# Quarters of the up weights by plain loads with their sums on VectorE, and the last pass's pairs one iteration later

## The chip, the cores and the metric

The kernel runs on one core of one Trainium2 chip. The metric is the device time of one execution in microseconds, the median of several runs. TensorE (PE) multiplies, VectorE (DVE) and ScalarE (ACT) do elementwise work, GpSimd (POOL) does small work and issues some DMAs, SyncE (SP) issues most DMAs.

## The reference

Two layers of a decoder trunk on 512 tokens with a model width of 1024, all in float32. Each layer adds a mixer of four branches (their projections, an indexer with sparse attention, an mLSTM, a gating unit, a short convolution) to `x`, and then an MLP with a hidden width of 4096:

```python
def squared_relu_mlp(h, w_up, w_down):
    return jnp.square(jax.nn.relu(h @ w_up)) @ w_down

def reference(x, ln_mix, w_in, ...):
    for l in range(DEPTH):
        h = rms_norm(x, ln_mix[l])
        x = x + hybrid_mixer(h, pos, w_in[l], ...)
        h = rms_norm(x, ln_mlp[l])
        x = x + squared_relu_mlp(h, w_up[l], w_down[l])
    return x
```

The change lies mostly in `h @ w_up`, with a small part in the projections of the mixer.

## The kernel before, in words

**Split products.** Every float32 matrix is split into a high part (`hi`, a copy to fp32r) and a low part (`lo`, the rest). A product takes three matmuls: high by high, high by low, low by high (`mm3`, L268). For weights, `split_w` (L258) does this: ScalarE copies the raw weights to `whi` and VectorE subtracts to get `wlo`. There are two raw buffers (tag `raw`) and three each of `whi` and `wlo` (`WB`, L34). A raw buffer is free for the next load when both parts are made.

**Order of the work.** The kernel is unrolled by a scheduler, which places each engine's instructions in one fixed queue by priority and by its own idea of when inputs are ready. Loads of weights, splits, sums and the copies out of PSUM have high priority, so they run as far ahead as buffers allow. On the chip each queue is run strictly in order: an instruction that waits holds up all behind it. A plain dependency for order alone can be added by hand (`tc.add_manual_dep` with `V._dep`): it fixes a place in the schedule and adds no wait of its own between instructions of one engine.

**The MLP.** `mlp` (L389) takes the 4096 hidden columns in four passes of 1024. A pass has an up stage of four iterations `t` (L489), each for 256 hidden columns, and a down stage. An up iteration is either plain (two chunks of 128 columns by `next_w`, L246, 48 products of 128x128 by 512 tokens, L498) or by seven products (`up_seven`, L417): the 2x2 blocks of weights and of `h` are combined as in Winograd's form of Strassen's scheme, so that seven half-sized products take the place of eight. `SEVEN` (L38) says which iterations of each pass are done so: (2, 3), (1, 3), (1, 3), (0, 2). In what follows such an iteration is called a pair.

**A pair.** The four quarters of the pair's weights are B11, B12, B21 and B22, each 128x512 floats (256 KB), in DRAM one behind the other. They and their sums stand in four buffers `R[0]` to `R[3]` (tag `cr`, six buffers of 128x1024 in all, L39 and L407), each with a lower and an upper half. Before the change, B11 is loaded twice, B22 twice, B21 once, all on SyncE's queue (L430), and B12 twice by DMAs on GpSimd's queue that add to what is already there (L428). VectorE makes two sums (L442, L449). `form` (L445) splits a buffer when its first product is due, multiplies, and VectorE and ScalarE combine the results in PSUM into `F` (L457 to L484). `F` is then combined again and split into `ah` and `al` (L506 to L513) for the down stage. The down stage (L531 to L745) uses the same six buffers: two for a chain of sums, two for B22, two for a sum of two blocks. Its first loads are tied to `early`, the last product of iteration 0 (L494). In passes 1 to 3 its results are added to partial sums in DRAM by GpSimd's DMAs (L568).

**The mixer's start.** The second projection (L930) leaves four PSUM banks, which ScalarE copies to `sm` and `qe`, eight copies with a factor `rs` (L933 to L937). Its results and those of the first projection (`qiT`, transposed at L975) share the same PSUM banks. Then comes the third projection, whose four chunks of weights are split by `next_w`.

Nearly all instructions show line 143, a helper that records them, so groups are told apart by the names of their tiles: `up` for products of the up stage, `q` and `r` for those of the down stage, `tk` for token projections, `cr` for the buffers above, `U` for the combinations in a pair, `co` for results of the down stage.

Of the kernel before, what the change touches and what calls it, by code (L numbers as in the profile page):

```python
# [16 lines left out]
AF = mybir.ActivationFunctionType  # L17
ALU = mybir.AluOpType
# [16 lines left out]
G1K = ((1, 1, 2, 2, 2), (2, 2, 2, 2))  # L35
KORD = ((0, 1, 2, 3, 4, 5, 6, 7), (4, 5, 6, 7, 0, 1, 2, 3))
PASSES = (8, 8, 8, 8)
SEVEN = ((2, 3), (1, 3), (1, 3), (0, 2))  # L38
CRB = 6  # L39
BIG = 1e30  # L40

# [12 lines left out]
def chunk_plan(l):  # L54
# [30 lines left out]
    for p, nt in enumerate(PASSES):  # L85

        half = nt // 2 * P
        for t in range(0, half, P):
            parts = 2 if t // P in SEVEN[p] else 1
            for i in range(parts):  # L90
# [76 lines left out]
def ins_of(r):  # L167
    return getattr(r, "ins", r)


def trunk(tc, x_in, wall, consts, lps, sgus, out):
    nc = tc.nc
    at = dict(mm=None, side=False, first=None)
    V, S, G, T_ = (Paced(tc, e, at) for e in (nc.vector, nc.scalar, nc.gpsimd, nc.tensor))
    HP = lambda off=URGENT: tc.high_priority(offset=off)
    plan = [ch for l in range(NL) for ch in chunk_plan(l)]
    with ExitStack() as es:
# [80 lines left out]
        def split_w(raw, L, n, copy=S.copy):  # L258
            hi = wpool.tile([P, WCH], F32R, name="whi", tag="whi", bufs=WB[1])
            lo = wpool.tile([P, WCH], F32R, name="wlo", tag="wlo", bufs=WB[1])  # L260
            with HP():
                copy(hi[:, :L], raw[:, :L])
                r = V.tensor_sub(lo[:, :L], raw[:, :L], hi[:, :L].bitcast(F32))
            at["first"] = r if pos[0] == 1 else None
            return (hi[:, :L].rearrange("p (k n) -> p k n", n=n),
                    lo[:, :L].rearrange("p (k n) -> p k n", n=n))
# [17 lines left out]
        side = []  # L284
# [104 lines left out]
        def mlp(l, hh, hl, r2, gain, fp, sh, sl):  # L389
# [9 lines left out]
            sums = sum_dram[l]  # L399
            with tc.tile_pool(name="ap", bufs=1) as ap:  # L400
# [6 lines left out]
                def cr():  # L407
                    return ap.tile([P, 1024], F32, name="cr", tag="cr", bufs=CRB)
# [8 lines left out]
                def up_seven(F):  # L417

                    base, sz = off[0], P * 512
                    off[0] += 4 * sz  # L420
                    pos[0] += 4

                    def ld(dst, i, j, add=False):
                        o = base + ((i - 1) * 2 + j - 1) * sz
                        src = wall[o:o + sz].rearrange("(p l) -> p l", l=512)
                        with HP():
                            if add:
                                nc.gpsimd.dma_start(dst, src, accum_op=ALU.add)  # L428
                            else:
                                nc.sync.dma_start(dst, src)  # L430

                    R = [cr() for _ in range(4)]
                    lo, up = slice(0, 512), slice(512, 1024)
                    ld(R[0][:, up], 1, 1)
                    ld(R[0][:, up], 1, 2, True)
                    ld(R[0][:, lo], 1, 1)
                    ld(R[1][:, up], 2, 2)
                    ld(R[2][:, lo], 2, 2)
                    ld(R[2][:, lo], 1, 2, True)
                    ld(R[3][:, lo], 2, 1)  # L440
                    with HP():
                        V.tensor_add(R[1][:, lo], R[0][:, up], R[1][:, up])  # L442
                    ws = [None] * 4

                    def form(f, o, i, n, first=True):  # L445
                        if ws[i] is None:
                            if i == 2:
                                with HP():
                                    V.tensor_add(R[2][:, up], R[1][:, lo], R[3][:, lo])  # L449
                            ws[i] = split_w(R[i], 512 if i == 3 else 1024, P)  # L450
                        w_h, w_l = ws[i]
                        for k in range(4):
                            bh, bl = moving(f, k)
                            mm3(o, w_h[:, 4 * n + k], w_l[:, 4 * n + k], bh, bl, first and k == 0, k == 3, not first)
                        tick()

                    A, B, C, E = (mmtile("up", "ms")[:, 0:256] for _ in range(4))  # L457
                    s1, s2 = (hpool.tile([P, 2, 256], F32, name="U", tag=n) for n in ("acc", "sq"))
                    U, U2, W, R5 = s1[:, 0], s1[:, 1], s2[:, 0], s2[:, 1]
                    form(A11, A, 0, 0)  # L460
                    with HP():
                        S.copy(U, A)
                    form(S1, B, 0, 1)
                    with HP():
                        S.copy(R5, B)
                    form(S2, C, 1, 0)
                    with HP():
                        V.tensor_sub(U2, C, U)
                    form(S4, B, 1, 1, False)
                    with HP():  # L470
                        V.tensor_add(F[:, A12], B, U2)
                    form(S3, C, 2, 0, False)
                    with HP():
                        V.tensor_sub(W, C, U)
                        V.tensor_add(F[:, A22], W, R5)
                        S.activation(F[:, 2:4], F[:, 2:4], AF.Relu)
                    form(A22, E, 2, 1)
                    with HP():
                        V.tensor_sub(F[:, A21], E, W)
                        S.activation(F[:, A21], F[:, A21], AF.Relu)  # L480
                    form(A12, A, 3, 0, False)
                    with HP():
                        S.activation(F[:, A11], A, AF.Relu)
                        S.activation(F, F, AF.Square)  # L484

                for p, nt in enumerate(PASSES):
# [44 lines left out]
                    nkp, base, sz = nk // 2, off[0], P * 1024  # L531
# [113 lines left out]
                    for k in range(nkp):  # L645
                        raw = wpool.tile([P, WCH], F32, name="raw", tag="raw", bufs=WB[0])
# [54 lines left out]
                    for k in range(nkp):  # L701
                        raw = wpool.tile([P, WCH], F32, name="raw", tag="raw", bufs=WB[0])
# [25 lines left out]
                    for b in range(2):  # L728
                        for qs in ((0,), (1,)) if final and b else ((0, 1),):
                            o = slice(qs[0] * 256, qs[-1] * 256 + 256)  # L730
# [5 lines left out]
                            c, a = c11[b][:, o], bank[b][:, o]  # L736
# [18 lines left out]
        for l in range(NL):  # L755
# [13 lines left out]
            if nxt:  # L769
                hh, hl = nxt  # L770
                rs, rb = rstd(acc, l + 1, 8)
# [3 lines left out]
def mixer(tc, em, env):  # L775
    nc = tc.nc
    HP = lambda off=URGENT: tc.high_priority(offset=off)
# [7 lines left out]
    def et(name):  # L785
        return yp.tile([P, T], F32, name=name, tag="e", bufs=8)
# [14 lines left out]
    if l > 0:  # L801
        rs, rb = env["rs"], env["rb"]
# [86 lines left out]
    else:  # L889
# [28 lines left out]
        rs, rb = rstd(acc[0], 0)  # L918
# [11 lines left out]
    psm = tok_proj(336, 2, range(4), ["mm", "ms", "ms", "ms"])  # L930
    sm = tt([P, 320], "sm").rearrange("p (c w) -> p c w", c=4)
    qe = [et("qe0"), et("qe1")]
    for c in range(4):  # L933
        with HP():
            S.activation(sm[:, c], psm[c][:, 0:80], AF.Identity, scale=rs[:, c:c + 1])
            S.activation(qe[c // 2][:, (c % 2) * 256:(c % 2) * 256 + 256], psm[c][:, 80:336], AF.Identity,
                         scale=rs[:, c:c + 1])  # L937
    rsh = tt([P, 4], "rsh")
    V.tensor_scalar(rsh, rs, 0.5, None, ALU.mult)

# [405 lines left out]
    for c in range(4):  # L1346
        with HP():
            S.activation(ke[c // 2][:, (c % 2) * 256:(c % 2) * 256 + 256], kvp[c][:, 0:256], AF.Identity,
                         scale=rs[:, c:c + 1])
# [38 lines left out]
    for c in range(4):  # L1388
        with HP():
            S.activation(v2[c // 2][:, (c % 2) * 256:(c % 2) * 256 + 256], pav[c][:, :256], AF.Identity,  # L1390
                         scale=rs[:, c:c + 1])
    vs = tt([P, 4], "vs")
    for c2 in range(2):
        t = et("gv")
        gelu2(v2[c2], t)
        for j in range(2):
            s_ = slice(j * 256, j * 256 + 256)
            c = c2 * 2 + j
# [202 lines left out]
```

## Time and profile before

| | |
|---|---|
| runs | 1639.28, 1639.61 and 1641.83 us, median 1639.61 |
| profiled execution | 1638.28 us, span 1636.5 us |
| granted TensorE clock | 0.991 |
| busy | PE 1588.2, DVE 1221.8, ACT 757.4, POOL 170.9 us |
| idle time of VectorE until a quarter landed | 89.7 us in 22 waits |
| DMA | 230.81 MB, mean 141 GB/s |

In a row of a group stand the line, engine, operation, out<-in with shapes and the count, then busy time in us and the mean duration in ns, then the engine's idle time just before these instructions and what ended it. In a row of a timeline stand the start and duration in us, and in brackets the idle time before and what ended it. In a row of waits stand who waited for whom, then us in total, times, and the longest. In a row of DMA issues stand count, KB each, and median us from issue to landing. SPq and POOLq are the queues that issue DMAs.

### The profile page before, as it was taken

The numbers are of one execution on the slowest core, as the hardware profiler recorded it, in microseconds if no ns is written. First come the engines' busy times: TensorE is split into PE (matmuls) and PEld (weight loads), VectorE is DVE, ScalarE is ACT, GpSimd is POOL, SyncE is SP. The second block draws the span as 40 slices with busy tenths as digits, with TensorE's granted clock in tenths as the row PEclk, the third lists the DMA queues.
The fourth block names the chain that finished last, engine by engine and source line by source line (L and its number), as shares of the span: only waits on it lengthen the run. The fifth ranks groups of instructions, "written<-read, shape, count | busy, mean of one in ns | idle before, by whom it ended". The sixth has DMA issues, their size and how long they took to land.

```text
span 1636.5 us, 22046 instructions
## 1 busy us (share of the span) xinstructions
PE 1588.2 (97%) x8163; PEld 1329.5 (81%) x8163; DVE 1221.8 (75%) x2095; ACT 757.4 (46%) x1168; POOL 170.9 (10%) x219
## 2 busy tenths in 40 slices
PE   9899999999998999989999999999999999989798
PEld 7788888888887787878888878878888788878687
DVE  6799997555578686766978999965556686857678
ACT  4554224423356474645545433254234564636363
POOL 1221000000001012121013110000000010021210
PEclk9999999999999999999999999999999999999999
DMA  7433322322366677768445233223223567686892
GB/s 176 135 89 109 101 96 97 117 96 93 110 185 174 186 187 171 202 149 259 133 126 149 79 111 104 81 97 132 97 88 127 160 189 202 165 174 167 167 283 78
DMA packets 85323, 230.81 MB, mean 141 GB/s; under 512 B 9664, under 2 KB 17024, under 8 KB 85216
## 3 DMA queue, kind: packets, MB, share of 16 engines
q1 hardware_dynamic: 63664, 179.74, 33.5%
q0 software_dynamic: 20688, 48.66, 15.9%
q8 instruction: 64, 1.05, 0.3%
q10 hardware_dynamic: 864, 1.01, 0.2%
q14 instruction: 43, 0.35, 0.1%
HBM read 204.69 MB, written 21.01 MB: 138 GB/s over the span
## 4 chain that ended last, share of the span: by engine, by line
PE 53%; DVE 21%; issue 11%; DMA 10%; ACT 4%; POOL 1%; SPq 0%; DVEq 0%; POOLq 0%; ACTq 0%
PE up L143 15%; PE g L143 14%; DMA cr<-in_wall_dram 7%; DVE wlo L143 6%; PE tk L143 6%; PE wo L143 4%; PE p L143 4%; PE q L143 3%; DVE sco L143 3%; PE fm L143 2%; PE r L143 2%; ACT whi L143 2%; DVE m L143 2%; DMA sum_dram<-co 1%; DVE Fs L143 1%
## 5 line engine op out<-in xcount | busy, mean ns | idle before, releaser
L143 ACT CAST whi<-raw 128x1024 fp32r<-128x1024 f32 (+3 forms) x204 | 224.2, 1100 | 224.0 <-DMA raw<-in_wall_dram 70.3
L143 DVE TENSOR_TENSOR wlo<-raw,whi 128x1024 fp32r<-128x1024 f32 (+3 forms) x205 | 262.8, 1283 | 32.4 <-ACT whi L143 30.3
L143 DVE TENSOR_TENSOR wlo<-cr,whi 128x1024 fp32r<-128x1024 f32 (+1 forms) x144 | 166.5, 1161 | 55.2 <-ACT whi L143 55.1
L143 PE MATMUL g<-hh,whi 128*128 128x512 f32 x512 | 200.6, 392 | 0.0
L143 PE MATMUL g<-hh,wlo 128*128 128x512 f32 x512 | 199.5, 390 | 0.0
L143 PE MATMUL g<-hl,whi 128*128 128x512 f32 x512 | 199.3, 389 | 0.0
L143 ACT CAST whi<-cr 128x1024 fp32r<-128x1024 f32 (+1 forms) x144 | 144.4, 1004 | 115.3 <-PE r L143 44.1
L143 PE MATMUL up<-hh,whi 128*128 128x512 f32 (+1 forms) x448 | 155.6, 347 | 5.2 <-DVE co L143 5.2
L143 PE MATMUL up<-hh,wlo 128*128 128x512 f32 (+1 forms) x448 | 155.1, 346 | 2.7 <-DVE wlo L143 2.7
L143 PE MATMUL up<-hl,whi 128*128 128x512 f32 (+1 forms) x448 | 155.0, 346 | 0.0
L143 ACT ACTIVATE gs<-gs 128x512 f32<-128x512 f32 x64 | 40.6, 634 | 201.3 <-DVE gs L143 201.2
L143 DVE TENSOR_TENSOR cr<-cr 128x512 f32<-128x512 f32 (+1 forms) x48 | 41.6, 867 | 95.5 <-DMA cr<-in_wall_dram 89.7
L143 PEld LDWEIGHTS g<-hh,wlo 128*128 128x128 f32 x512 | 96.1, 188 | 20.5
L143 PEld LDWEIGHTS g<-hh,whi 128*128 128x128 f32 x512 | 96.1, 188 | 19.8 <-issue 0.2
L143 PEld LDWEIGHTS g<-hl,whi 128*128 128x128 f32 x512 | 96.2, 188 | 19.1
L143 PE MATMUL tk<-whi,hh 128*128 128x512 f32 (+2 forms) x304 | 108.7, 361 | 0.0
L143 PE MATMUL tk<-wlo,hh 128*128 128x512 f32 (+2 forms) x304 | 107.7, 356 | 0.0
L143 PE MATMUL tk<-whi,hl 128*128 128x512 f32 (+2 forms) x304 | 106.8, 354 | 0.0
L428 POOL DMA_DIRECT2D cr<-in_wall_dram x32 | 28.1, 879 | 720.5 <-DMA cr<-in_wall_dram 567.8
L143 DVE TENSOR_TENSOR gs<-g,rb 128x512 f32<-128x512 f32 x64 | 44.1, 689 | 78.8 <-PE g L143 78.7
L143 PE MATMUL q<-wlo,ah 128*128 128x512 f32 (+1 forms) x260 | 100.1, 389 | 0.7 <-DVE wlo L143 0.7
L143 PE MATMUL q<-whi,ah 128*128 128x512 f32 (+1 forms) x260 | 100.5, 392 | 0.0
(309 smaller groups left out, 3759.6 us busy)
## 6 DMA issues: line engine op xcount, KB each, us to landing
raw<-in_wall_dram SPq DMA_DIRECT2D x131, 512.0 KB, 3.9
raw<-in_wall_dram SPq DMA_DIRECT2D x64, 640.0 KB, 3.8
cr<-in_wall_dram POOLq DMA_DIRECT2D x48, 512.0 KB, 7.2
cr<-in_wall_dram SPq DMA_DIRECT2D x80, 256.0 KB, 4.1
cr<-in_wall_dram SPq DMA_DIRECT2D x32, 512.0 KB, 4.3
cr<-in_wall_dram POOLq DMA_DIRECT2D x32, 256.0 KB, 4.5
sum_dram<-co POOLq DMA_DIRECT2D x32, 256.0 KB, 7.3
x<-in_x_dram SPq DMA_DIRECT2D x16, 256.0 KB, 5.0
```

Of the source, the lines that this page charges most:

```text
L143: r = f(*a, **k)
L428: nc.gpsimd.dma_start(dst, src, accum_op=ALU.add)
```

## The change

- The four quarters of a pair are loaded once each, plainly, on SyncE's queue. Nothing is accumulated by a DMA.
- VectorE makes all four sums of a pair: B11+B12, that plus B22, B12+B22, and the sum of all four, each just ahead of the split of the buffer that it fills. Before, it made two of them.
- The quarters lie in other halves: B11 in the first buffer, B12 and B21 in the second, B22 in the third, in the order in which the buffers are asked for. The fourth holds sums alone.
- In the last pass the pairs are iterations 1 and 2 instead of 0 and 2. The packed order of the weights in DRAM follows `SEVEN` on the host.
- In the mixer, the last of the eight copies out of PSUM is kept in `hold`, and the copy of the next `split_w` is scheduled behind it on ScalarE.

```diff
-SEVEN = ((2, 3), (1, 3), (1, 3), (0, 2))
+SEVEN = ((2, 3), (1, 3), (1, 3), (1, 2))
...
             with HP():
-                copy(hi[:, :L], raw[:, :L])
+                c = copy(hi[:, :L], raw[:, :L])
+                if at["hold"] is not None:
+                    tc.add_manual_dep(ins_of(c), ins_of(at["hold"]).name, V._dep, reason="order")
+                    at["hold"] = None
                 r = V.tensor_sub(lo[:, :L], raw[:, :L], hi[:, :L].bitcast(F32))
...
                     R = [cr() for _ in range(4)]
+                    R[1:] = R[2:] + R[1:2]
                     lo, up = slice(0, 512), slice(512, 1024)
-                    ld(R[0][:, up], 1, 1)
-                    ld(R[0][:, up], 1, 2, True)
-                    ld(R[0][:, lo], 1, 1)
-                    ld(R[1][:, up], 2, 2)
-                    ld(R[2][:, lo], 2, 2)
-                    ld(R[2][:, lo], 1, 2, True)
-                    ld(R[3][:, lo], 2, 1)
-                    with HP():
-                        V.tensor_add(R[1][:, lo], R[0][:, up], R[1][:, up])
+                    B11, S1w, S2w, B22 = R[0][:, lo], R[0][:, up], R[1][:, lo], R[1][:, up]
+                    S3w, all4, B21, B12 = R[2][:, lo], R[2][:, up], R[3][:, lo], R[3][:, up]
+                    ld(B11, 1, 1)
+                    ld(B12, 1, 2)
+                    ld(B22, 2, 2)
+                    ld(B21, 2, 1)
+                    sums = {0: ((S1w, B11, B12),), 1: ((S2w, S1w, B22),), 2: ((S3w, B12, B22), (all4, S2w, B21)), 3: ()}
                     ws = [None] * 4
 
                     def form(f, o, i, n, first=True):
                         if ws[i] is None:
-                            if i == 2:
+                            for o_, a_, b_ in sums[i]:
                                 with HP():
-                                    V.tensor_add(R[2][:, up], R[1][:, lo], R[3][:, lo])
+                                    V.tensor_add(o_, a_, b_)
                             ws[i] = split_w(R[i], 512 if i == 3 else 1024, P)
...
             S.activation(sm[:, c], psm[c][:, 0:80], AF.Identity, scale=rs[:, c:c + 1])
-            S.activation(qe[c // 2][:, (c % 2) * 256:(c % 2) * 256 + 256], psm[c][:, 80:336], AF.Identity,
-                         scale=rs[:, c:c + 1])
+            env["at"]["hold"] = S.activation(qe[c // 2][:, (c % 2) * 256:(c % 2) * 256 + 256], psm[c][:, 80:336],
+                                             AF.Identity, scale=rs[:, c:c + 1])
```

More of the change, by code (lines that the diff above doesn't have):

```diff
@@ L172, in trunk @@
     nc = tc.nc
-    at = dict(mm=None, side=False, first=None)
+    at = dict(mm=None, side=False, first=None, hold=None)
     V, S, G, T_ = (Paced(tc, e, at) for e in (nc.vector, nc.scalar, nc.gpsimd, nc.tensor))
@@ L421, in up_seven, with ld @@
                     pos[0] += 4
-                    def ld(dst, i, j, add=False):
+                    def ld(dst, i, j):
                         o = base + ((i - 1) * 2 + j - 1) * sz
-                        src = wall[o:o + sz].rearrange("(p l) -> p l", l=512)
                         with HP():
[L427 to L430, printed above, removed]
+                            nc.sync.dma_start(dst, wall[o:o + sz].rearrange("(p l) -> p l", l=512))
                     R = [cr() for _ in range(4)]
+                    R[1:] = R[2:] + R[1:2]
                     lo, up = slice(0, 512), slice(512, 1024)
-                    ld(R[0][:, up], 1, 1)
-                    ld(R[0][:, up], 1, 2, True)
-                    ld(R[0][:, lo], 1, 1)
-                    ld(R[1][:, up], 2, 2)
-                    ld(R[2][:, lo], 2, 2)
-                    ld(R[2][:, lo], 1, 2, True)
-                    ld(R[3][:, lo], 2, 1)
-                    with HP():
-                        V.tensor_add(R[1][:, lo], R[0][:, up], R[1][:, up])
+                    B11, S1w, S2w, B22 = R[0][:, lo], R[0][:, up], R[1][:, lo], R[1][:, up]
[5 more added lines that the diff above has]
+                    sums = {0: ((S1w, B11, B12),), 1: ((S2w, S1w, B22),), 2: ((S3w, B12, B22), (all4, S2w, B21)), 3: ()}
                     ws = [None] * 4
```

## The prediction

> **What bounds the kernel now.** I read the page first, then who TensorE waited for, then how much of each stage it stood idle, and last the order on VectorE, SyncE and ScalarE around those idle stretches.
>
> ```profile
> span 1636.5 us, 22046 instructions
> PE 1588.2 (97%) x8163; PEld 1329.5 (81%) x8163; DVE 1221.8 (75%) x2095; ACT 757.4 (46%) x1168; POOL 170.9 (10%) x219
> ```
>
> TensorE is busy for 1588.2 of 1636.5 us, and the change neither adds nor removes a matmul (two iterations of each pass stay in seven products). So there are at most 48.3 us of idle TensorE to win, plus what a slow clock stretches behind an idle stretch. The waits of TensorE say where the idle time lies (total, times, longest, in us):
>
> ```profile
> PE up L143 <- DVE U L143: 13.3, 6, 3.6
> PE up L143 <- ACT U L143: 8.9, 4, 2.7
> PE up L143 <- DVE co L143: 5.2, 2, 3.7
> PE qiT L143 <- ACT qe L143: 5.0, 1, 5.0
> ```
>
> 27.4 us of it are waits of the up products for VectorE or ScalarE, 5.0 us is one wait in the first mixer. By stage (window, its length, then busy time of PE, PEld, DVE, ACT and POOL, the granted clock, the DMA share and GB/s); the first rows are pass 0, its down stage, and the up stages of passes 1, 2 and 3 of layer 0, the last four the up stages of layer 1; the windows of passes 2 and 3 in layer 1, and of pass 3 in layer 0, begin in the tail of the down stage before:
>
> ```profile
> 492.00:520.00 28.00, 23.20 (x171) 22.42 (x170) 22.16 (x35) 17.03 (x26) 5.41 (x7) 0.88 0.73 181
> 520.00:560.00 40.00, 39.52 (x173) 31.61 (x172) 30.06 (x33) 20.46 (x25) 2.56 (x3) 1.00 0.63 175
> 560.00:603.00 43.00, 41.75 (x261) 37.70 (x261) 30.48 (x43) 26.40 (x38) 5.36 (x7) 1.00 0.77 207
> 640.00:688.00 48.00, 44.75 (x275) 39.99 (x274) 31.24 (x43) 26.55 (x38) 8.80 (x11) 1.00 0.88 210
> 722.00:767.00 45.00, 40.11 (x241) 36.44 (x242) 27.26 (x38) 22.00 (x32) 10.93 (x14) 0.92 0.88 219
> 1299.00:1325.00 26.00, 22.10 (x168) 21.35 (x167) 21.78 (x34) 16.84 (x26) 4.83 (x7) 0.93 0.70 182
> 1365.00:1409.00 44.00, 42.71 (x266) 38.28 (x265) 31.09 (x43) 26.59 (x38) 5.31 (x7) 1.00 0.74 204
> 1442.00:1499.00 57.00, 51.42 (x291) 45.58 (x290) 34.41 (x46) 27.74 (x39) 11.39 (x14) 0.94 0.80 199
> 1529.00:1579.00 50.00, 41.33 (x257) 36.38 (x256) 32.10 (x44) 22.94 (x32) 11.48 (x14) 1.00 0.89 220
> ```
>
> Length less PE gives the idle time: pass 0 has 4.8 and 3.9 us (layers 0 and 1), pass 1 has 1.25 and 1.29, pass 2 has 3.25 and 5.58, pass 3 has 4.89 and 8.67: 33.6 us in all, against 0.5 us in the down stage of 520 to 560.
>
> **Why these stages stand still.** The timeline of VectorE in pass 0, then SyncE and GpSimd in the same stretch:
>
> ```profile
> 488.16 1.42 DVE L143 TENSOR_TENSOR cr<-cr 128x512 f32<-128x512 f32 x2 [8.88 <-DMA cr<-in_wall_dram]
> 494.57 1.23 DVE L143 TENSOR_TENSOR al<-Fs,ah 128x1024 fp32r<-128x1024 f32 x1
> 498.75 0.69 DVE L143 TENSOR_TENSOR cr<-cr 128x512 f32<-128x512 f32 x1 [2.95 <-DMA cr<-in_wall_dram]
> 499.36 1.22 DVE L143 TENSOR_TENSOR wlo<-cr,whi 128x1024 fp32r<-128x1024 f32 x1
> ```
>
> ```profile
> 476.32 4.50 SPq L430 DMA_DIRECT2D cr<-in_wall_dram  x8
> 490.74 4.21 SPq L430 DMA_DIRECT2D cr<-in_wall_dram  x2
> 479.89 0.96 POOL L428 DMA_DIRECT2D cr<-in_wall_dram  x1 [227.90 <-DMA cr<-in_wall_dram]
> ```
>
> A sum (cr<-cr) stands in VectorE's queue and waits for a quarter to land; the split behind it (wlo at 499.36) belongs to the pair that TensorE is multiplying, and TensorE waits for that. Over the whole run:
>
> ```profile
> DVE cr L143 <- DMA cr<-in_wall_dram: 89.7, 22, 8.9
> cr<-in_wall_dram SPq DMA_DIRECT2D x80, 256.0 KB, 4.1
> cr<-in_wall_dram POOLq DMA_DIRECT2D x32, 256.0 KB, 4.5
> L143 DVE TENSOR_TENSOR cr<-cr 128x512 f32<-128x512 f32 x32 | 22.1, 692 | 95.5 <-DMA cr<-in_wall_dram 89.7 <-DVE U L143 4.3 <-issue 1.4
> ```
>
> **The change, part by part.** *Loads.* A pair of seven products took five plain loads (16 x 5 = 80) and two accumulating ones (16 x 2 = 32). An accumulating load can start only when the plain one below it has landed: 4.1 + 4.5 = 8.6 us in series. Now four plain loads go out on SyncE, 4.1 us each and overlapping; 48 of 112 transfers go (12.6 MB), and on GpSimd's queue nothing of the up stage is left ahead of the stores of sums and of the down stage's accumulating loads.
>
> *Sums.* Four instead of two to a pair: 32 more at 0.692 us = 22.1 us of VectorE, in the two stretches of a pass where it is fullest.
>
> *Buffers.* All loads of a pair now lie in the first three of its four buffers; the fourth (S3 and the sum of all) is only written by VectorE. The sum of all (`all4`) therefore no longer waits for a load into the buffer that comes free last.
>
> *Pass 0* (pairs 2 and 3 side by side). The wait of 8.88 us to 488.16 is for an accumulated quarter, the wait of 2.95 us to 498.75 for the load that SyncE could issue last (the second of the two at 490.74 to 494.95). Six quarters now need no buffer of the running pair; they are among SyncE's first loads at 476.32, eight of which took 4.50 us. The first two land at about 480.5 (476.32 + 4.1) and not at 488, so the first split can be up to 7 us earlier, its buffer goes back earlier by as much, and the second pair's two other quarters land before VectorE comes to them. Both waits go. At stake: the idle 4.8 + 3.9 = 8.7 us, and a slow clock worth at most (1 - 0.88) x 28 = 3.4 and (1 - 0.93) x 26 = 1.8 us, of which I take half (part of it falls into idle time): 11.3 us. What is late next is VectorE itself: 22.16 us busy in a window that shrinks from 28 to about 23, plus 4 x 0.692 = 2.8 us, that is 25. The sums can go into the 8.88 us that it idled before, and its trailing work into the down stage, which has 9.9 us free (40 less 30.06). Left of the wait: between 0 and 2.8 us a layer; I take 1.2. **Gain 9 us.**
>
> The longest wait of TensorE in that window of layer 0 is this one:
>
> ```profile
> PE up L143 <- ACT U L143: 2.6, 1, 2.6
> ```
>
> So the clock fell to 0.88 behind waits of at most 2.6 us, while pass 2 of layer 0, with 3.25 us idle, kept 1.00. The Trainium skill ("TensorE: Matmul & The Clock Gate", Part 1) says that the clock halves after an idle window of about 3.4 us. The rows differ from that as a threshold, and I go by the rows; by that rule pass 0 would give back idle time alone, 6.3 us instead of 9.
>
> *Pass 2.* Here the order of the wait stays. VectorE, then SyncE:
>
> ```profile
> 648.27 1.23 DVE L143 TENSOR_TENSOR wlo<-cr,whi 128x1024 fp32r<-128x1024 f32 x1 [0.44 <-ACT whi L143]
> 650.83 1.23 DVE L143 TENSOR_TENSOR wlo<-cr,whi 128x1024 fp32r<-128x1024 f32 x1 [1.33 <-ACT whi L143]
> 657.69 0.69 DVE L143 TENSOR_TENSOR cr<-cr 128x512 f32<-128x512 f32 x1 [5.63 <-DMA cr<-in_wall_dram]
> 649.53 2.89 SPq L430 DMA_DIRECT2D cr<-in_wall_dram  x2
> ```
>
> The second pair's B22 needs the buffer that the first split (ending 649.50) frees, and goes out at 649.53 as now; B21 can follow at once instead of 2.56 us later (at 649.53 + 2.89 - 0.33 = 652.09), behind the second split. Its sums come up to 2.2 us sooner, but there are three at this place instead of one (2 x 0.692 = 1.4 us more), and behind them on VectorE stand the next split and the subtractions that free TensorE's banks. Bounds: 1.4 us lost to 3.25 and 5.58 us gained; I take 1 us a layer, by the nearest row: **gain 2 us.** *Pass 1* has 2.5 us at stake and keeps its first wait (the second quarter still needs the last chain buffer of the down stage): between 1 lost and 1 gained, **nothing**.
>
> *Pass 3* (pairs 0 and 2 become 1 and 2). Its first iteration, 48 products at 0.23 us = 11 us, now needs only plain weights, so the quarters have that long more, as in passes 1 and 2. In exchange the pairs are neighbours. On SyncE the plain chunks' loads move ahead of the quarters; nothing else changes places there. The last pair stays in iteration 2, so the tiles it holds come free as before. The chain buffers for the down stage come free some 10 us later; the plain fourth iteration (11 us) and the first 24 products of the down stage (5.5 us) cover that, and pass 0, which has no plain iteration there, lost 0.5 us in its down stage. Pass 3 has 13.6 us idle, plus half of (1 - 0.92) x 45 = 3.6: 15.4. It then resembles pass 2, 8.8 us idle plus half of (1 - 0.94) x 57 = 3.4, less the 2 above: 8.5, plus 1 us a layer for the neighbours. **Gain 5 us**, between 0 and 11.
>
> *The hold.* The next split's copy on ScalarE, which is that of the first chunk of the third projection, must now follow the last of the eight copies out of PSUM (sm, qe). ScalarE in layer 0, TensorE there, ScalarE in layer 1:
>
> ```profile
> 31.08 1.05 ACT L143 CAST whi<-raw 128x1024 fp32r<-128x1024 f32 x1 [2.01 <-PE tk L143]
> 43.80 1.04 ACT L143 CAST whi<-raw 128x1024 fp32r<-128x1024 f32 x1 [11.67 <-DMA raw<-in_wall_dram]
> 46.67 0.52 ACT L143 ACTIVATE qe<-tk,rs 128x256 f32<-128x256 f32 x1
> ```
>
> ```profile
> 38.19 0.39 PE L143 MATMUL tk<-whi,hh 128*128 128x512 f32 x1
> 38.42 0.40 PE L143 MATMUL tk<-wlo,hh 128*128 128x512 f32 x1
> 46.07 1.12 PE L143 MATMUL qiT<-cst,qr 128*128 128x128 f32 x4 [4.98 <-ACT qe L143]
> ```
>
> ```profile
> 844.10 1.05 ACT L143 CAST whi<-raw 128x1024 fp32r<-128x1024 f32 x1 [2.90 <-PE tk L143]
> 851.97 0.33 ACT L143 ACTIVATE sm<-tk,rs 128x80 f32<-128x80 f32 x1 [0.22 <-PE tk L143]
> 852.20 0.47 ACT L143 ACTIVATE qe<-tk,rs 128x256 f32<-128x256 f32 x1
> ```
>
> Today the first chunk's copy runs early (31.08, 844.10). In layer 0 it is the *second* chunk's copy, waiting 11.67 us for its load, that blocks qe and TensorE. If the second copy stays behind the first, qe runs at about 39, the first chunk is whole after 1.05 + 1.22 us more, and TensorE waits 3 us instead of 5: gain 2 us. In layer 1, which loses nothing today, the first copy starts at 852.7 instead of 844.10, and TensorE, done with the projection before at about 851.9, waits to 853.7 for it and to about 855 for its low part: 3 us lost. **Lost: 1 us.** Behind the held copy queue only later copies of chunks.
>
> **Sum.** 9 + 2 + 5 - 1 = 15 us off the profiled execution's 1638.28 us (its span 1636.5 and 1.8 around it) is 1623.3; the median of the runs shown is 1639.61, 1.3 more. The removed 12.6 MB should shorten landings in all these stages, which I count with 2 us. Forecast for the median: 1638.3 - 17 + 1.3, or **1622 us**.
>
> **Rivals.**
> *The hold turns against the kernel.* Nothing holds the second chunk's copy; where a load that was expected early put it ahead of qe, it can stay ahead. Then qe still ends at 47.2, the first chunk is copied only at 48.2 and whole at 49.4, and TensorE waits 11 us from 38.19 instead of 5: 6 lost in layer 0, 3 in layer 1, 8 more than I took. 1622 + 8 = 1630. For it: the row at 43.80; against: the copies share three buffers and otherwise stand in order. Chance 0.25.
> *The buffers are the limit.* In passes 1 to 3 quarters wait for buffers, not for accumulation, and only pass 0 gains: 1639.6 - 9 + 1 = 1632. Chance 0.08. Together with the first rival, 1640, no change: 0.07.
> *All waits of the up stages go:* 33.6 us idle less about 3: 1609. For it: every one follows a sum that waits. Chance 0.10.
> *Slower: VectorE becomes the bound of the pairs.* If each added sum runs ahead of a split for which TensorE is waiting, all 22.1 us are on the path; with pass 0's 9 us gained, 1639.6 + 22.1 - 9 = 1653. It decides when VectorE carries a backlog from pair to pair: pass 0, without its idle time, leaves it 1.0 us (28 - 4.8 - 22.16) for 2.8 us of sums. Against: in passes 1 to 3 it idles 12.5 to 22.6 us of a window. Chance 0.08.
>
> **How the numbers follow.** The forecast keeps 0.42. Under 0.2% (3.3 us) is about what a measurement cannot tell from no change. Faster: 0.42 + 0.25 + 0.08 + 0.10 = 0.85; same 0.07; slower 0.08. From 1609 (all waits gone) to 1636 (the hold, with pass 3 gaining nothing) the range leaves out the slow rivals and part of the best case.
>
> **What would show it.** Right: no accumulating up load on GpSimd; VectorE's waits of cr for loads well under 89.7 us; windows of pass 0 nearly full; the tail before pass 3 without the waits for co; 64 sums of 0.69 us. Wrong: PE idle at the first mixer over 5 us, or a wait at the third projection of layer 1 well over 3 us (the hold); wlo or U late in windows where VectorE is busy throughout (VectorE the bound); DVE cr still waiting in pass 0.

## The result and the profile after

The changed kernel takes 1603.2 us (median of 1601.55 to 1607.95), the kernel before beside it 1640.72 us (1639.28 to 1644.25). The ratio is 0.9773, 95% interval [0.9746, 0.9800]: 37 us faster, where 17 were forecast, and below the low end of the range. All ratios here are of fast runs: one run of e11 below (1728.1 us, at a clock of 0.85) was slow and is left out. The profiled execution took 1603.06 us, its span is 35.2 us shorter than before. From the page of the changed kernel, its span and busy times:

```profile
span 1601.3 us, 21951 instructions
PE 1576.8 (98%) x8163; PEld 1322.8 (83%) x8163; DVE 1238.7 (77%) x2127; ACT 756.9 (47%) x1168; POOL 144.0 (9%) x187
```

The same 8163 matmuls; TensorE stands idle for 24.5 us where it was 48.3. Its busy time is 11.4 us less too, with a mean granted clock of 0.998 where it was 0.991. Who TensorE waited for:

```profile
PE up L143 <- DVE U L143: 8.9, 4, 2.8
PE q L143 <- ACT F L143: 4.2, 3, 1.6
PE tk L143 <- ACT whi L143: 3.9, 3, 1.7
```

The waits for `co` (5.2 us) and for ScalarE's `U` (8.9 us) are gone, and so is the wait of 5.0 us for `qe`. New are `q` for `F` and `tk` for `whi`. The up stages as windows (passes 0 to 3 of layer 0, then of layer 1), from each stage's first product to the next stage's:

```profile
463.90:506.80 42.90, 42.90 (x281) 38.67 (x280) 37.35 (x59) 27.97 (x42) 3.80 (x5) 1.00 0.61 181
545.60:588.30 42.70, 42.36 (x265) 38.13 (x264) 31.60 (x44) 26.67 (x38) 4.53 (x6) 1.00 0.69 197
627.10:670.80 43.70, 42.22 (x266) 38.22 (x264) 29.62 (x42) 26.63 (x38) 7.91 (x10) 1.00 0.78 191
709.60:756.80 47.20, 42.82 (x265) 38.15 (x263) 28.71 (x42) 25.69 (x37) 7.97 (x10) 1.00 0.82 216
1259.60:1302.60 43.00, 43.00 (x282) 38.74 (x281) 37.60 (x59) 28.09 (x43) 3.82 (x5) 1.00 0.57 171
1341.40:1383.30 41.90, 41.90 (x265) 38.14 (x264) 29.45 (x41) 25.72 (x37) 4.49 (x6) 1.00 0.69 199
1422.10:1468.00 45.90, 43.69 (x265) 39.69 (x264) 30.28 (x43) 26.63 (x38) 7.87 (x10) 0.96 0.75 184
1506.80:1553.20 46.40, 43.92 (x265) 39.58 (x263) 28.41 (x41) 25.71 (x38) 7.93 (x10) 0.96 0.83 221
```

Pass 0 has no idle TensorE left, and its clock is 1.00, where it was 0.88 and 0.93 in the second half of the stage. Pass 3 is the one with most left: 4.4 and 2.5 us. In the timeline of the changed kernel, pass 0 of layer 0, first VectorE, then SyncE:

```profile
473.66 0.69 DVE L143 TENSOR_TENSOR cr<-cr 128x512 f32<-128x512 f32 x1 [0.49 <-DMA cr<-in_wall_dram]
477.42 1.29 DVE L143 TENSOR_TENSOR cr<-cr 128x512 f32<-128x512 f32 x2 [3.07 <-DMA cr<-in_wall_dram]
478.63 1.22 DVE L143 TENSOR_TENSOR wlo<-cr,whi 128x1024 fp32r<-128x1024 f32 x1
```

```profile
470.21 1.75 SPq L429 DMA_DIRECT2D cr<-in_wall_dram  x4
472.48 7.72 SPq L429 DMA_DIRECT2D cr<-in_wall_dram  x4
```

All eight quarters of both pairs are under way within 10 us, the two sums ahead of the first split are made at 477.42 (before at 488.16, while the stage itself begins only 6.1 us earlier), and no sum waits any more once the pairs run. Over the whole run (who VectorE waited for, the loads, the sums):

```profile
DVE cr L143 <- DMA cr<-in_wall_dram: 60.1, 16, 7.7
cr<-in_wall_dram SPq DMA_DIRECT2D x64, 256.0 KB, 3.4
L143 DVE TENSOR_TENSOR cr<-cr 128x512 f32<-128x512 f32 (+1 forms) x80 | 61.7, 793 | 60.4 <-DMA cr<-in_wall_dram 60.1
```

VectorE still waits 60 us for quarters (before 89.7), but TensorE's waits for the `U` of VectorE behind them are down from 13.3 to 8.9 us, and those for `co` are gone. Landings of 256 KB fell from 4.1 to 3.4 us.

Where the 35.2 us of span went, by the first product of each stage in both traces: the up stages of pass 0 -12.9 us, of pass 1 -2.8, of pass 2 -3.5, of pass 3 -0.9; the down stages of passes 0 to 2 -13.9, of pass 3 +3.2; the first mixer's start -4.5, the second's +2.7; the rest of the two mixers, which the change doesn't touch and whose length varies by 1.6 (layer 0) and 2.5 us (layer 1) over all traces, -2.3. The table has these lengths in us (layer 0 / layer 1) for the kernels that the next section explains; the last down stage of layer 1 includes the end of the kernel, and "again" is a second execution of the changed kernel.

| stage | before | after | again | e14 | e1 | e13 | e5 | e10 | e16 |
|---|---|---|---|---|---|---|---|---|---|
| mixer's start | 63.9/57.8 | 59.4/60.5 | 61.6/60.2 | 59.8/58.0 | 64.2/57.8 | 64.2/58.1 | 61.6/60.5 | 59.1/60.3 | 61.4/60.5 |
| up 0 | 50.2/48.6 | 43.0/42.9 | 42.9/42.9 | 42.9/42.9 | 43.7/42.9 | 45.6/47.4 | 47.2/43.5 | 46.2/46.9 | 42.9/42.9 |
| down 0 | 39.4/39.9 | 38.8/38.8 | 38.9/38.8 | 38.8/38.8 | 38.8/38.8 | 38.8/38.8 | 38.8/38.8 | 38.8/38.8 | 38.8/38.8 |
| up 1 | 43.6/43.8 | 42.7/41.9 | 41.9/41.9 | 41.9/41.9 | 41.9/41.9 | 43.6/43.4 | 43.2/42.6 | 41.9/41.9 | 41.9/41.9 |
| down 1 | 39.2/42.7 | 38.8/38.8 | 38.8/38.8 | 38.8/38.8 | 38.8/38.8 | 38.8/38.8 | 38.8/38.8 | 38.8/38.8 | 38.8/38.8 |
| up 2 | 45.7/47.3 | 43.7/45.9 | 44.6/46.1 | 45.7/43.5 | 47.0/44.1 | 42.1/47.6 | 50.4/51.9 | 48.1/46.1 | 47.5/46.8 |
| down 2 | 41.0/44.6 | 38.8/38.8 | 38.8/38.8 | 39.9/38.9 | 38.8/38.8 | 40.1/41.8 | 38.8/38.8 | 38.8/38.8 | 38.8/38.8 |
| up 3 | 48.3/46.3 | 47.2/46.4 | 45.3/45.8 | 44.6/43.5 | 45.5/43.4 | 46.7/44.4 | 50.7/50.6 | 44.1/48.4 | 47.2/46.7 |
| down 3 | 40.2/46.6 | 42.0/48.1 | 41.7/48.5 | 40.2/46.6 | 40.2/47.0 | 40.2/47.2 | 41.6/48.5 | 42.0/48.8 | 41.6/48.1 |

A single length is good to about 2 us in the first mixer and in passes 2 and 3, up to 4 in pass 2 (e8 and e14 are one kernel: 43.5/47.7 and 45.7/43.5 in pass 2); in passes 0 and 1 and in the down stages it mostly repeats within 1 us. So the ratios decide, and the table says where.

### The profile page after: what moved, and what is told of

The parts are those of the page before. It is cut to its first block, busy times and chain, and to the rows that moved or that the text cites. A ratio compares the mean times of both kernels' runs of the same rounds, so it can differ in the third digit from the quotient of the medians.

```text
span 1601.3 us, 21951 instructions
## 1 busy us (share of the span) xinstructions
PE 1576.8 (98%) x8163; PEld 1322.8 (83%) x8163; DVE 1238.7 (77%) x2127; ACT 756.9 (47%) x1168; POOL 144.0 (9%) x187
## 4 chain that ended last, share of the span: by engine, by line
PE 73%; DVE 13%; issue 5%; ACT 4%; DMA 4%; POOL 0%; SPq 0%; DVEq 0%; ACTq 0%; POOLq 0%
PE g L143 18%; PE up L143 15%; PE tk L143 8%; PE r L143 6%; PE fm L143 6%; PE wo L143 5%; PE q L143 5%; PE p L143 5%; DVE wlo L143 4%; ACT whi L143 2%; DVE sco L143 2%; DMA cr<-in_wall_dram 2%; DMA raw<-in_wall_dram 1%; DVE Fs L143 1%; DVE cr L143 1%
## 5 line engine op out<-in xcount | busy, mean ns | idle before, releaser
L143 DVE TENSOR_TENSOR cr<-cr 128x512 f32<-128x512 f32 (+1 forms) x80 | 61.7, 793 | 60.4 <-DMA cr<-in_wall_dram 60.1
L143 DVE TENSOR_TENSOR gs<-g,rb 128x512 f32<-128x512 f32 x64 | 44.1, 689 | 78.7 <-PE g L143 78.6
L143 PE MATMUL q<-whi,al 128*128 128x512 f32 (+1 forms) x260 | 99.8, 389 | 0.0
```

The lines of the kernel that those rows point to most:

```text
L143: r = f(*a, **k)
```

## The experiments

**The three parts, each alone.** *e1_loads* has the new loads, sums and buffers, with the old pairs and no hold (as an edit of the changed kernel):

```diff
-SEVEN = ((2, 3), (1, 3), (1, 3), (1, 2))
+SEVEN = ((2, 3), (1, 3), (1, 3), (0, 2))
...
-            env["at"]["hold"] = S.activation(qe[c // 2][:, (c % 2) * 256:(c % 2) * 256 + 256], psm[c][:, 80:336],
+            S.activation(qe[c // 2][:, (c % 2) * 256:(c % 2) * 256 + 256], psm[c][:, 80:336],
```

> The changed loads and sums alone: pairs of the last pass at 0 and 2 as before, no hold. If the loads and sums carry the gain (my theory now): 1640 - 30, about 1610 us, with pass 0 of both layers near 43 us and the tails of the down stages gone. If the later pairs of the last pass carry the down tails before it: 1620 or more, with the down stages before pass 3 still near 41 and 44.6 us.

1603.66 us, 0.9791 [0.9774, 0.9809]: by the ratios all but 3 us of the gain lie in the loads, sums and buffers, and the intervals allow all of it.

*e2_hold* is the kernel before with the hold alone (the diff's lines in `trunk`, `split_w` and the second projection).

> Before plus the hold alone. If the hold works as the profile of after suggests: 4.5 us gained in the first mixer, 2.7 lost in the second, 1639 us by the median; if the 1.3 and 1.0 us that the gate stages gained come with it too: 1636.5 us. By my rival that the second chunk's copy stays ahead: 1648 us.

1630.26 us, 0.9956 [0.9940, 0.9973], 7 us. By stages the hold gives 4.6 in layer 0 and costs 2.7 in layer 1, about 2 net; the other 5 us lie in stages that it doesn't touch, and stay open.

*e3_pairs* is the kernel before with the later pairs alone.

```diff
-SEVEN = ((2, 3), (1, 3), (1, 3), (0, 2))
+SEVEN = ((2, 3), (1, 3), (1, 3), (1, 2))
```

> Before plus the last pass's pairs at 1 and 2 alone, with the accumulating loads kept. As I forecast (pass 3 turns into a pass like pass 2): 5 us gained, 1635 us. If the later pairs crowd the loads of the down stage behind them, as the profile of after shows (waits of q for F): 1 us or less gained, 1639 to 1645 us, with the down stage of pass 3 longer by 1.5 us or more.

1634.63 us, 0.9993 [0.9973, 1.0013]: no difference. The up stage of pass 3 goes from 48.3/46.3 to 46.7/48.0 us, the down stage behind it from 40.2/46.6 to 41.6/48.4.

*e4_hold_l0* is the changed kernel with the hold in layer 0 only, *e8_best* that with the old pairs too.

```diff
-            env["at"]["hold"] = S.activation(qe[c // 2][:, (c % 2) * 256:(c % 2) * 256 + 256], psm[c][:, 80:336],
+            env["at"]["hold" if l == 0 else "held"] = S.activation(qe[c // 2][:, (c % 2) * 256:(c % 2) * 256 + 256], psm[c][:, 80:336],
```

> After, with the hold in layer 0 alone. The projection stage of layer 1 goes back from 60.5 to 57.8 us and nothing else changes: 2.7 us under after, 1600.5 us. If the order of later work hangs on it too, other stages move by over 1 us.

> After, with the pairs of the last pass at 0 and 2 as before, and the hold in layer 0 alone. If the later pairs cost about 3.5 us a layer and the hold 2.7 us in layer 1: 1603 - 7 - 2.7, about 1594 us. If the later pairs are worth something with the new loads: 1600 us or more.

e4: 1600.01 us, 0.9780 [0.9753, 0.9807], with the second mixer's start back at 57.8 us; by the ratio this can't be told from the changed kernel (0.9773). e8: 1597.18 us, 0.9748 [0.9714, 0.9783]. In the changed kernel, ScalarE in layer 0, then TensorE in both layers:

```profile
38.54 0.47 ACT L143 ACTIVATE qe<-tk,rs 128x256 f32<-128x256 f32 x1
38.90 1.04 ACT L143 CAST whi<-raw 128x1024 fp32r<-128x1024 f32 x1
44.08 1.05 ACT L143 CAST whi<-raw 128x1024 fp32r<-128x1024 f32 x1 [4.13 <-DMA raw<-in_wall_dram]
```

```profile
40.00 1.20 PE L143 MATMUL tk<-whi,hh 128*128 128x512 f32 x4 [1.72 <-ACT whi L143]
835.10 1.20 PE L143 MATMUL tk<-whi,hh 128*128 128x512 f32 x4 [1.72 <-ACT whi L143]
```

The second chunk's copy stays behind the first and no longer stands ahead of `qe`. TensorE waits 1.7 us in each layer: four products of the high part run first, so that the low part's 1.2 us is covered.

**Inside the loads: which buffer comes last.** *e13_b21_early* is the kernel before, with its accumulating loads and its two sums, but B21 lies in the second buffer asked for, ahead of the third sum's quarters, and the third sum in the last:

```diff
                     R = [cr() for _ in range(4)]
+                    R[1:] = R[2:] + R[1:2]
...
                     ld(R[1][:, up], 2, 2)
+                    ld(R[3][:, lo], 2, 1)
                     ld(R[2][:, lo], 2, 2)
                     ld(R[2][:, lo], 1, 2, True)
-                    ld(R[3][:, lo], 2, 1)
```

> Before, accumulating loads and two sums kept, with one thing of the change: B21 in the second buffer, loaded ahead of the third sum's quarters, so that the sum of all does not wait for the buffer that comes free last. If that buffer is the main cause in passes 1 to 3: 10 to 20 us under before, about 1622 us. If the accumulating loads are: within 5 us of before, since the last buffer now takes a plain and an accumulating load in series.

1615.97 us, 0.9842 [0.9826, 0.9859]: 26 us from the places of the loads alone (B21 moves from the last buffer to the second, and the two buffers between move one back). Who VectorE waited for, and the one waiting sum that falls into pass 2's up stage of layer 0 (637.0 to 679.1):

```profile
DVE cr L143 <- DMA cr<-in_wall_dram: 59.6, 14, 9.0
```

```profile
648.48 0.69 DVE L143 TENSOR_TENSOR cr<-cr 128x512 f32<-128x512 f32 x1 [2.10 <-DMA cr<-in_wall_dram]
```

This is the sum of all of the second pair. In the kernel before it waited 5.63 us for B21, at 657.69. In the changed kernel, pass 2 of layer 0, SyncE and then VectorE:

```profile
619.41 0.85 SPq L429 DMA_DIRECT2D cr<-in_wall_dram  x2
631.07 0.33 SPq L429 DMA_DIRECT2D cr<-in_wall_dram  x1
```

```profile
637.85 0.69 DVE L143 TENSOR_TENSOR cr<-cr 128x512 f32<-128x512 f32 x1 [6.81 <-DMA cr<-in_wall_dram]
639.71 1.29 DVE L143 TENSOR_TENSOR cr<-cr 128x512 f32<-128x512 f32 x2
```

B12 and B21 go out together while the stage before still runs, B22 follows, the second sum waits for B22, and the third sum and the sum of all behind it wait for nothing. Told apart by their order in VectorE's queue, the waits for quarters are these: before, 47.8 us at sums of all (14 waits) and 41.9 at second sums (8); in e13, 8.6 and 51.0; in the changed kernel none at a sum of all.

*e5_b21_last* does the reverse in the changed kernel: plain loads and four sums, but B21 alone in the buffer that comes last.

```diff
-                    R[1:] = R[2:] + R[1:2]
+                    R[1], R[2] = R[2], R[1]
...
-                    S3w, all4, B21, B12 = R[2][:, lo], R[2][:, up], R[3][:, lo], R[3][:, up]
+                    S3w, all4, B21, B12 = R[2][:, lo], R[2][:, up], R[3][:, lo], R[2][:, up]
```

> After, with B12 in the second, B22 in the third and B21 alone in the fourth buffer: four plain loads and four sums as in after, but the sum of all waits again for the buffer that comes free last. If the buffers carry the gain in passes 1 to 3: up stages of passes 2 and 3 longer by 1 to 3 us each, 8 us over after, 1611 us, pass 0 unchanged at 43 us. If not: within 2 us of after.

1630.29 us, 0.9960 [0.9939, 0.9982]: 33 us over e8 on the same chip and, by the ratios (0.9960 - 0.9773), some 30 over the changed kernel, where 8 were expected. Nearly all the gain is gone though nothing is accumulated. Who TensorE and VectorE waited for, then VectorE in pass 2's up stage of layer 0:

```profile
PE up L143 <- DVE U L143: 23.5, 8, 4.9
PE up L143 <- DVE wlo L143: 4.9, 4, 2.1
```

```profile
DVE cr L143 <- DMA cr<-in_wall_dram: 91.7, 24, 9.9
```

```profile
648.48 1.29 DVE L143 TENSOR_TENSOR cr<-cr 128x512 f32<-128x512 f32 x2 [8.71 <-DMA cr<-in_wall_dram]
653.59 0.69 DVE L143 TENSOR_TENSOR cr<-cr 128x512 f32<-128x512 f32 x1 [2.68 <-DMA cr<-in_wall_dram]
```

The first row waits for B22, as in the changed kernel (there 6.81 us); the second is the sum of all, which waits again for B21. Behind both on VectorE stand splits and the combinations `U` that free TensorE's banks. Over the run the sums of all wait 22.0 us, in 8 waits. Passes 2 and 3 lose 3 to 7 us each, and pass 0 of layer 0 loses 4, which was not expected.

**Inside the loads: the accumulation.** *e10_acc* makes B11+B12 by a plain and an accumulating load again, *e16_acc3* does that for B12+B22 and loads it last; the rest is the changed kernel, with the other sums on VectorE. The four plain loads of a pair stay, so each has two loads more than the changed kernel. The edit of e10:

```diff
+                    ld(S1w, 1, 1)
+                    ld(S1w, 1, 2, True)
...
-                    sums = {0: ((S1w, B11, B12),), 1: ((S2w, S1w, B22),), 2: ((S3w, B12, B22), (all4, S2w, B21)), 3: ()}
+                    sums = {0: (), 1: ((S2w, S1w, B22),), 2: ((S3w, B12, B22), (all4, S2w, B21)), 3: ()}
```

> After, with B11+B12 alone made by the DMA again (plain load, then an accumulating load on GpSimd's queue), the three other sums on VectorE: five plain loads and one accumulating one, three sums. If the serial accumulating load is what holds VectorE: pass 0 goes back by 2 to 7 us in each layer and the down tails come back in part, 1612 to 1625 us. If bytes are the cause: about 1608 us, spread evenly. If VectorE's sums are the bound of after: faster than after, under 1600 us.

> The changed kernel, but the third sum (B12+B22) is made by a plain load and an accumulating DMA on GpSimd's queue, as before the change; its two loads stand last. If the accumulating load of the third sum is what makes the down stages of passes 1 and 2 wait, those stages grow from 38.8 us by 1 to 5 us each and the kernel takes 1610 us or more. If it is not, the down stages stay within 0.3 us of 38.8, and what is lost is lost in the up stages, by the wait for that load.

e10: 1620.55 us, 0.9888 [0.9855, 0.9921], some 18 us lost by the ratios, 3 to 4 in each pass 0. VectorE in pass 0 of layer 0 again has the wait for the two loads in series, ahead of the pair's first split:

```profile
481.59 1.30 DVE L143 TENSOR_TENSOR cr<-cr 128x512 f32<-128x512 f32 x2 [8.43 <-DMA cr<-in_wall_dram]
482.81 1.22 DVE L143 TENSOR_TENSOR wlo<-cr,whi 128x1024 fp32r<-128x1024 f32 x1
```

e16: 1609.56 us, 0.9830 [0.9798, 0.9862], 7.6 us over the changed kernel on the same chip, mostly in the up stages of passes 2 and 3; VectorE's waits for quarters grow from 60.1 to 76.1 us. The down stages stay at 38.8 us, so this load alone is not what made them wait. From e13 (0.9842) to e1 (0.9791), which drops both accumulations and makes the sums on VectorE, it is 0.5%, 8 us.

**VectorE, bytes, GpSimd's queue.** *e9_sums* makes two of the four sums twice. *e6_bytes* and *e11_bytes_pool* bring back the bytes: three quarters of a pair are loaded once more into a tile that nothing reads, one on SyncE and two on GpSimd, or all on GpSimd. *e12_pool_wait* lets GpSimd's queue wait for two quarters of each pair, by stores of 16x8 numbers. The main lines of e9, e11 and e12, in this order:

```diff
                                     V.tensor_add(o_, a_, b_)
+                                    if o_ is S1w or o_ is S3w:
+                                        V.tensor_add(o_, a_, b_)
...
+                    for i in range(3):
+                        d = ap.tile([P, 496], F32, name="spare", tag="spare")
+                        with HP():
+                            nc.gpsimd.dma_start(d, wall[base + i * sz:base + i * sz + sz].rearrange("(p l) -> p l", l=512)[:, :496])
...
+                    for q in (B11, B22):
+                        n = at["spare"] = at.get("spare", -1) + 1
+                        with HP():
+                            nc.gpsimd.dma_start(spare[n], q[0:16, 0:8])
```

> After, with two of the four sums of each pair made twice on VectorE: 32 sums of 0.69 us more, 22.1 us. If VectorE were the bound of the pairs (my slower rival): most of the 22 us on the path, 1620 us or more. If its time there is free: within 4 us of after, 1600 to 1607 us.

> After, with three more plain loads to a pair (each of nearly a quarter, into a spare tile that nobody reads; one on SyncE's queue, two on GpSimd's): the bytes and issues of before without its sums in the DMA. If fewer bytes carry the gain of the down tails (14 us over all down stages): these come back, 1603 + 10 to 14, about 1615 us. If the serial accumulating load carries it: within 3 us of after.

> After, with three spare loads to a pair, of nearly a quarter each, all on GpSimd's queue and none on SyncE's (whose queue stood still behind them in the run before): the bytes of before. If bytes make the gain: 1612 us or more, the down stages of passes 1 and 2 over 40 us. If not: within 5 us of after.

> After, with two tiny stores to a pair (512 bytes each, nobody reads them) on GpSimd's queue, each of which waits for a quarter to land as the accumulating loads did. If the stores of partial sums that stood behind these waits made the tails of the down stages: tails of passes 1 and 2 back by 2 to 6 us each, 1612 us or so. If not: within 3 us of after.

e9: 1607.58 us, 0.9795 [0.9777, 0.9812], within the interval of the changed kernel. Its page has the added work:

```profile
PE 1579.1 (98%) x8163; PEld 1325.7 (83%) x8163; DVE 1259.3 (79%) x2159; ACT 756.8 (47%) x1168; POOL 144.0 (9%) x187
L143 DVE TENSOR_TENSOR cr<-cr 128x512 f32<-128x512 f32 (+1 forms) x112 | 82.1, 763 | 49.6 <-DMA cr<-in_wall_dram 49.4
```

VectorE has 20.6 us more to do, and 10.8 us of that are taken off its idle time in front of the sums (60.4 to 49.6). e6: 1631.41 us, 0.9958 [0.9937, 0.9978], but it says nothing about bytes. Who the queues waited for:

```profile
SPq L443 <- DMA spare<-in_wall_dram: 122.9, 19, 10.0
```

The spare load on SyncE waited for its tile, and all later loads stood behind it. e11, which leaves SyncE alone, takes 1609.52 us, 0.9817 [0.9773, 0.9862] with 230.41 MB moved. By the ratios the bytes cost 7 us, but its interval overlaps that of the changed kernel ([0.9746, 0.9800]), so it may be nothing or twice that. e12: 1605.35 us, 0.9780 [0.9756, 0.9804]: no difference, though GpSimd's queue waits 700.0 us for quarters in 32 waits.

**Two parts taken back, beside the changed kernel.** *e14_best* is e8 again, *e15_after* the changed kernel, on one chip.

> The changed kernel with two parts taken back: the pairs of the last pass are iterations 0 and 2 again, and the ordering of ScalarE's copies is kept in layer 0 only. Run beside the changed kernel on the same chip. If the later pairs cost 3 to 7 us and the ordering costs layer 1 about 2.7 us, it takes about 1597 us, some 6 less than the changed kernel. If the two differ by less than 2 us on one chip, neither part can be told from no change, and only the loads matter.

> The changed kernel itself, on the same chip as the version with two parts taken back. If the later pairs and the ordering in layer 1 cost time, about 1603 us and some 6 more than that version. If they don't, the two are equal within 2 us.

1594.03 us, 0.9723 [0.9694, 0.9752], against 1601.94 us, 0.9781 [0.9754, 0.9808]: 8 us. The intervals don't overlap. By the table, 6.4 us of it are pass 3 with its down stage, and 2.2 us the second mixer's start. (e1, which has the old pairs too, shows the same in the lengths of pass 3, but not in its ratio of 0.9791, taken on another chip.) In the changed kernel, pass 3 of layer 0, SyncE, then ScalarE, then TensorE:

```profile
743.05 0.33 SPq L543 DMA_DIRECT2D raw<-in_wall_dram  x1
```

```profile
754.29 1.05 ACT L143 CAST whi<-raw 128x1024 fp32r<-128x1024 f32 x1 [7.42 <-DMA raw<-in_wall_dram]
755.24 1.04 ACT L143 CAST ah<-Fs 128x1024 fp32r<-128x1024 f32 x1
756.19 0.59 ACT L143 ACTIVATE F<-up 128x512 f32<-128x512 f32 x1
```

```profile
756.83 0.50 PE L143 MATMUL q<-whi,ah 128*128 128x512 f32 x1 [1.65 <-ACT F L143]
```

With the pairs one iteration later, the raw weights of the down stage go out at 743.05, while the DMA is busy for 0.82 of the stage, and the copy on ScalarE that needs them starts 11.2 us later, after a wait of 7.42 us. Behind it on ScalarE stands `F`, for which the down stage waits.

## Why the prediction was wrong

The sign was right, and the wait that was named as the kernel's bound (a sum behind which a split or `U` stands). The size was not: 17 us forecast, 37 measured. Two steps failed: the ends of the down stages were no term of the sum, and the place of B21 was priced in passes 0 and 2 alone. In the profiled executions, against the terms of the sum: down stages of passes 0 to 2, nothing forecast, 13.9 gained; pass 0, 9 and 12.9; passes 1 and 2, 2 and 6.3; pass 3 with its down stage, 5 gained forecast, 2.3 lost; the hold, 1 lost forecast, 1.8 gained. (The sum itself comes to 1622.6 and not 1622.) By its own steps:

- **"Here the order of the wait stays", gain 2 us in pass 2, nothing in pass 1.** This step failed. It had B21 go out behind B22 and the split of the first pair, and took 1 us a layer. In the trace B22 does go out behind that split (631.07), but B21 went out with B12 at 619.41, so the sum of all waits for no load. In pass 2 of layer 0 that sum is ready 13.9 us into the stage instead of 15.9, about the bound of 2.2 us that the step gave; what it missed is that the same wait stood in other stages too (12.1 of the 47.8 us lie in the up stages of pass 2). That `all4` "no longer waits for a load into the buffer that comes free last" was priced besides only in pass 0, as one of the two waits there, and not in passes 1 and 3 or at the ends of the down stages. The places of the loads alone are 26 us by the ratio (e13), 20.7 between the two profiled executions, and undoing them costs some 30 (e5). By e13's table it falls on pass 0 (5.7 us), on the down stages of passes 0 to 2 (9.6), and on passes 1 to 3 (7.3).
- **The down stages of passes 0 to 2: 13.9 us, no term of the sum.** The windows of passes 2 and 3 held these tails, and their idle time went into the step on the pairs ("It then resembles pass 2") instead of the one on the loads. In the kernel before, the tail of pass 2 in layer 1: VectorE, TensorE, GpSimd and SyncE:

```profile
1528.87 0.69 DVE L143 TENSOR_TENSOR cr<-cr 128x512 f32<-128x512 f32 x1 [3.22 <-DMA cr<-in_wall_dram]
1540.97 0.69 DVE L143 TENSOR_TENSOR cr<-cr 128x512 f32<-128x512 f32 x1 [5.49 <-DMA cr<-in_wall_dram]
1542.72 1.41 DVE L143 SCALAR_TENSOR_TENSOR co<-r,t,Z 128x512 f32<-128x512 f32 x2
```

```profile
1543.61 0.36 PE L143 MATMUL up<-hh,whi 128*128 128x256 f32 x1 [3.65 <-DVE co L143]
```

```profile
1532.65 0.86 POOL L428 DMA_DIRECT2D cr<-in_wall_dram  x1 [6.98 <-DVE co L143]
1533.19 2.06 POOL L568 DMA_DIRECT2D sum_dram<-co  x2
```

```profile
1534.38 0.33 SPq L430 DMA_DIRECT2D cr<-in_wall_dram  x1
```

- The next up stage can't start until VectorE has copied `co` out. `co` stands behind two sums that wait: a sum of all, 3.22 us for B21, and a second sum, 5.49 us for the B22 issued at 1534.38, beside an accumulating load and two stores that GpSimd's queue let go within 2.6 us. The changed kernel has the same pattern one pass earlier, with the wait over in time:

```profile
1419.77 0.69 DVE L143 TENSOR_TENSOR cr<-cr 128x512 f32<-128x512 f32 x1 [3.29 <-DMA cr<-in_wall_dram]
1421.52 1.40 DVE L143 SCALAR_TENSOR_TENSOR co<-r,t,Z 128x512 f32<-128x512 f32 x2
```

- Which part of the change removes these waits is open in part. The down stages come down to 38.8 us with plain loads whatever the buffers (e5) and with either accumulation alone (e10, e16). With both accumulations in the new buffers (e13) two thirds of the loss are gone: the sums of all no longer wait there, while the second sum at the same place still waits, 5.96 us. The bytes (e11) bring back little and waits of GpSimd's queue (e12) nothing. That the clump of transfers makes the quarter late is argued, not shown.
- **Pass 0, gain 9 us.** Measured 12.9. Both waits went, as said, and the clock came back whole. The 2.4 us kept back for the added sums were not needed: e9's 20.6 us more of VectorE cost nothing that can be told. The slow clock was counted by half, 2.6 us; besides the 8.7 us of idle time, TensorE's busy time in the two stages fell by 4.2. The Trainium skill's rule ("TensorE: Matmul & The Clock Gate", Part 1), that the clock halves after an idle window of about 3.4 us, would have left the clock out; the trace differs from it, since the longest waits there were 2.6 and 2.7 us.
- **Pass 3, gain 5 us.** Wrong in sign where it counts: on the old loads the later pairs do nothing (e3), on the new ones they cost about 6 (e14 beside e15). "The plain fourth iteration and the first 24 products of the down stage cover that" overlooked ScalarE, where a copy that waits for a late raw load stands ahead of `F`.
- **The hold, lost 1 us.** Right in layer 1 (3 said, 2.7 measured). In layer 0 the gain is 4.5, not 2 (2.3 in the second execution): of the 5 us of wait 1.7 is left, since the high part's products cover the low part. Net 1.8 gained, or nothing by the second execution. The rival in which the second copy stays ahead didn't happen.
- **2 us for the bytes.** No row stood behind this term. Landings are 0.7 us shorter; the worth of the bytes is 7 us by the ratio of e11, with an interval that holds nothing, so the term is neither confirmed nor refuted.
- **The rivals.** "The buffers are the limit" had the right subject and the wrong sign: it took the buffers as unchanged by the change. "All waits of the up stages go" (1609) came nearest in time, but 10.9 us of idle TensorE remain in the windows above; the rest came from tails and clock. VectorE as the bound is refuted by e9.

## What to carry to other kernels

Where a combination needs several loads and several sums in an in-order queue, ask which load stands in the buffer that comes free last, and whether a sum waits for it. Taking B21, for which the last sum waited, out of that buffer was worth 26 of 37 us here, although the third sum's loads took its place (e13); a last buffer that takes no load at all, but only what VectorE computes, is worth some 8 more (e16, which has two loads more). The bytes (7 us by the ratio, or nothing) and VectorE's added work (nothing that can be told) counted for less. In an in-order queue, ask of each instruction that waits for a load what stands behind it (a split, `U`, `co`, `F`), and price that wait in every stage in which the pattern recurs, the tails of other stages included. A change of several parts can hide a losing part: the version with the new loads, the old pairs and the hold in one layer takes 0.9723 of the time instead of 0.9781.

## What the runs showed of the hardware

In the kernel before, the clock in pass 0 of layer 0 is 0.50 from 500.8 to 507.6, right behind a wait of 2.6 us, and 1.00 from 507.6 to 520: the mean of 0.88 is one short stretch at half speed. The length of a wait alone does not decide it: behind the wait of 3.64 us that ends at 1472.16 the clock is 0.50 (1473.6 to 1477), behind that of 3.65 us to 1543.61 it stays at 1.00 (1543.6 to 1560). When the waits of pass 0 went, TensorE's busy time in its two stages fell by 4.2 us for the same products, so some of what looked like TensorE's work was an after-effect of idle time. One spare load per pair that waits for its tile at the head of SyncE's queue (e6: 122.9 us in 19 waits) undid most of the gain of the change, while the same 230.41 MB with the spare loads on GpSimd's queue alone (e11) cost 7 us by the ratios, or nothing.
